# A decoder layer on one core: long GpSimd work moved to VectorE, substitution by columns, attention blocks in lockstep

## The chip, the cores and the metric

The kernel runs on one core of one Trainium2 chip. The metric is device time in microseconds (us) of one execution. A core has five engines that work from queues of their own, each strictly in its program's order: TensorE (PE, matmuls; PEld is its weight load), VectorE (DVE), ScalarE (ACT), GpSimd (POOL) and SyncE (SP, which issues all DMAs here). They wait for each other on semaphores. Matmuls write to PSUM; everything else lies in SBUF or in device memory.

## The reference

One layer on 1024 tokens of width 1024, all in float32: a half-weighted SwiGLU block, a token mixer, a second SwiGLU block, a final RMSNorm. The mixer is what matters here:

```python
qa, ka, va, qkv_b, beta_raw, decay_raw, gdn_gate, gate_a, gate_b = jnp.split(h @ w_in, offsets, axis=-1)
# branch A: 12 heads of 64, three groups: window/dilation (128,1) (512,4) (2048,16), blocks of 128 queries
s = jnp.einsum('brnqhd,brnkhd->brnhqk', qb, kw) * (Dh ** -0.5)   # masked band
p = jnp.exp(s - m); l = jnp.sum(p, axis=-1, keepdims=True)
o = jnp.einsum('brnhqk,brnkhd->brnqhd', p / l, vw); lse = m + jnp.log(l)
wts = jax.nn.softmax(jnp.stack(lses, axis=0), axis=0)            # mixes the three groups
# branch B: 8 heads of 128, causal conv of 4 taps, silu, l2norm of q and k, then in chunks:
M = jnp.where(tri_strict, jnp.einsum('bhnid,bhnjd->bhnij', kbeta, kc) * decay, 0.0)
sol = lax.linalg.triangular_solve(M + jnp.eye(C), rhs, left_side=True, lower=True, unit_diagonal=True)
v_new = u_i - w_i @ state;  o_i = q_i @ state + a_i @ v_new      # scan over the chunks
state = state * sd_i + k_i^T @ v_new
ob = rmsnorm(ob, gdn_out_norm) * jax.nn.silu(gdn_gate)
merged = sigmoid(gate_a) * (ya @ w_branch_a) + sigmoid(gate_b) * (yb @ w_branch_b); return merged @ w_out
```

## The kernel before, in words

The stages run one after the other: first feed-forward (0 to 735 us), mixer (735 to 1930), merge of the branches and w_out (1930 to 2110), second feed-forward (2110 to 2878). Long products are made from pairs of a rounded high part and a low part: a weight tile arrives by DMA in `wraw`, ScalarE casts it to `wH` (L181), and the low part `wL` = `wraw` - `wH` is made on L182. Each product of 128 output columns by 512 tokens takes 24 matmuls of 128x512 (L204, in `proj`). In the mixer `C.pool_split` sends the low parts of the DeltaNet heads and gates to GpSimd, 48 tiles; the others go to VectorE.

The mixer is one long stream of such projections, 3072 long matmuls, into which everything else is woven. `Weave` keeps a planned time: `fill` adds 0.23 for each long matmul, and as soon as 2.07 (`STRETCH`, nine of them) have passed since the last poll, `poll` runs every task whose due time is reached. A task is a generator; the number that it yields is its delay until its next step. Matmuls keep this order on PE (`keep_in_program_order`). On the other engines a list scheduler places the instructions, by bands of priority: attention first, then heads 0 to 7, and the bulk (casts and low parts) last. PE therefore has one fixed order, and if an operand is late, all of PE waits.

What is woven in:

- `attention_block`, 48 blocks (3 groups, 2 pairs of heads, 8 blocks). Step one: two score products (L772), masked row maximum on VectorE (L774), exponential on ScalarE (L779). Step two, 2.07 later: transposes (L787) and their copies. Step three, 2.07 later: product with the values (L799), copy to the tile `o`, DMA to device memory. A block's first step is due 10.0 + 3.8 b after its projections.
- `combine`, eight times: reads the three groups' outputs back, mixes them on VectorE (L830 to L845), transposes on PE (L849) 9 planned us later.
- For each head of branch B: `gdn_conv` (L899 to L902, four taps: one on ScalarE, three on VectorE), `by_token` (transposes L908, squares L918, sums L919), `gdn_decay` (the masks D, L974 to L977), `gdn_solve`, `gdn_values` and `gdn_scan` over eight chunks of 128 (L1187: product with the state, L1189: subtraction on VectorE, L1191, L1197, L1202: state update on VectorE, nine long matmuls between turnarounds), `gdn_output` (L1224 to L1229).
- `rsqrt_cols` makes an inverse square root by three Newton steps. In the mixer three callers hand it `nc.gpsimd`: norms of keys and queries and the output norm, 32 calls. On GpSimd a step is four operations (L163, L168, L169, L170), on VectorE three (L163, L165, L166).
- `gdn_solve` inverts the unit lower triangles. `gdn_inverse_blocks` stores the diagonal 32x32 blocks of N and reads them back as `M`, one block per lane in four copies that each take eight columns, so that all 32 blocks of a head are inverted at once: entry i of a column is the sum of the entries before it times `M`'s entries i, one multiply and one sum per i (L1061 and L1062 for 1 to 15 in both halves at once, L1066 and L1067 for 16 to 31). The result goes out and back by DMA and is transposed (L1077). `gdn_merge` joins the blocks (L1097 to L1121). Its first product is due 51 planned us (`INVERSE` - 5) after the key products; before it, two scalings of the keys (L1022) run on GpSimd.

```python
def poll(self):
    while self.tasks and self.tasks[0][0] < self.now + 0.05:
        task = heapq.heappop(self.tasks)[2]
        delay = next(task, None)
```

Of the kernel before, what the change touches and what calls it, by code (L numbers as in the profile page):

```python
# [16 lines left out]
P = 128  # L17
T = 1024
# [64 lines left out]
STRETCH = 2.07  # L83


class Weave:
# [3 lines left out]
    def __init__(self, tc):  # L90
        self.tc, self.now, self.tasks, self.n, self.busy, self.last = tc, 0.0, [], 0, False, 0.0

# [664 lines left out]
def attention_block(C, q, k, g, hp, V, b):  # L757
# [7 lines left out]
    with band(C, "att"):  # L765
        o = C.mx.tile([P, 132], F32, name="o", tag="o", bufs=3)
        nm = C.mx.tile([P, 2], F32, name="nm", tag="nm", bufs=3)
        S = []
        for h in range(2):
            rows = slice(h * 64, h * 64 + 64)  # L770
            ps = psum(C, "tC")
            pe(nc.tensor.matmul(ps[:, :nk], q[rows, b * P:b * P + P], k[rows, k0:k0 + nk], start=True, stop=True), nk * 0.0017)  # L772
            s = C.mx.tile([P, 256], F32, name="s", tag="sc", bufs=7)
# [7 lines left out]
    yield STRETCH  # L781
    with band(C, "att"):
        pTs = []
        for h in range(2):
# [3 lines left out]
            pT = C.mx.tile([P, 256], F32, name="pT", tag="sc", bufs=7)  # L788
# [5 lines left out]
    yield STRETCH  # L794
# [16 lines left out]
    C.blocks -= 1  # L811


def combine(C):

    nc = C.nc
    while C.blocks:
        yield 1.0
    yield 4.0
    for t in range(NT):  # L820
        while sum(not X.vals[1] for X in C.heads) > 1:
            yield 1.0
        oc = C.tp.tile([P, 792], F32, name="oc", tag="xs", bufs=2).rearrange("p (g q f) -> p g q f", g=3, q=2)
# [15 lines left out]
        y = C.mx.tile([P, 256], F32, name="cy", tag="sc", bufs=7)  # L839
# [3 lines left out]
        yv = y.rearrange("p (q f) -> p q f", q=2)  # L843
        nc.vector.tensor_tensor(out=yv, in0=oc[:, 0, :, 0:128], in1=oc[:, 1, :, 0:128], op=ALU.add)
        nc.vector.tensor_tensor(out=yv, in0=yv, in1=oc[:, 2, :, 0:128], op=ALU.add)  # L845
        yield 9.0
        ps = psum(C, "tA")
        for f in range(2):
            C.weave.pe(nc.tensor.transpose(ps[:, f * P:f * P + P], y[:, f * P:f * P + P], C.ident), 0.11)  # L849
        yT = C.mx.tile([P, 2, P], F32, name="yT", tag="sc", bufs=7)  # L850
# [31 lines left out]
def gdn_conv(C, w_in, c0, ti, X, out, then):  # L882
# [6 lines left out]
    for q in (0, 1):  # L889
# [13 lines left out]
        C.weave.add(in_band(C, X.band, then(q)), 7.0)  # L903
# [34 lines left out]
def gdn_queries(C, w_in, X):  # L938
    X.q = t4c(C, "ka")

    def then(q):
        by_token(C, X, X.q, q, 8, None)
        if q:
            rs, _ = rsqrt_cols(C, X.ssq[:, 8:16], 1.0, EPS, 8, "rg", C.nc.gpsimd, 24)
# [10 lines left out]
def gdn_decay(C, X):  # L955
# [4 lines left out]
    while X.prev and not (X.prev.vals[1] and X.prev.A):  # L960
        yield 0.6
    segs = []
# [16 lines left out]
    X.D = D  # L979
# [17 lines left out]
def gdn_solve(C, X):  # L997
# [5 lines left out]
    rs, sv = rsqrt_cols(C, X.ssq[:, 0:8], 1.0, EPS, 8, "rg", nc.gpsimd, 24)  # L1003
# [17 lines left out]
    for dst, sc in ((kg, C.eG[:, :, h]), (X.kd, ks)):  # L1021
        nc.gpsimd.tensor_tensor(out=dst, in0=X.kd, in1=sc.unsqueeze(2).to_broadcast([P, NT, P]), op=ALU.mult)  # L1022
# [13 lines left out]
def gdn_inverse_blocks(C, X):  # L1036
# [11 lines left out]
    nc.vector.memset(M[:, 0:T:33], 1.0)  # L1048
    Tb = C.mx.tile([P, 288], F32, name="fsT", tag="fsT", bufs=1)
    pr = C.mx.tile([P, 128], F32, name="fsP", tag="fsP", bufs=1)  # L1050
# [5 lines left out]
    for i in range(1, 32):  # L1056
        n = i + 1
        if i < 16:
            mv = Mh[:, :, i:i + 32 * i + 1:32].unsqueeze(2).to_broadcast([P, 2, 4, n])
            v = pr[:, :8 * n].rearrange("p (h x j) -> p h x j", h=2, x=4)  # L1060
            nc.vector.tensor_tensor(out=v, in0=Th[:, :, :, 0:n], in1=mv, op=ALU.mult)  # L1061
            nc.vector.tensor_reduce(out=Th[:, :, :, i], in_=v, axis=AX.X, op=ALU.add)  # L1062
        else:
            mv = M[:, i:i + 32 * i + 1:32].unsqueeze(1).to_broadcast([P, 4, n])
            v = pr[:, :4 * n].rearrange("p (x j) -> p x j", x=4)
            nc.vector.tensor_tensor(out=v, in0=Tx[:, 0:4, 0:n], in1=mv, op=ALU.mult)  # L1066
            nc.vector.tensor_reduce(out=Tx[:, 0:4, i], in_=v, axis=AX.X, op=ALU.add)  # L1067
# [13 lines left out]
def gdn_merge(C, X, Tm, Um):  # L1081
# [13 lines left out]
    for lo, hi in quads:  # L1095
        for c in range(NT):
            pe(nc.tensor.matmul(ps[hi, c * 32:c * 32 + 32], N[lo, c, hi], Tm[lo, c, lo], start=True, stop=True), 0.055)  # L1097
        nc.vector.tensor_copy(W[hi], ps[hi, :256].rearrange("p (c t) -> p c t", t=32))
    yield STRETCH
    ps = psum(C, "tM")  # L1100
    for lo, hi in quads:
        for c in range(NT):
            pe(nc.tensor.matmul(ps[hi, c * 32:c * 32 + 32], Um[hi, c, hi], W[hi, c, :], start=True, stop=True), 0.055)
        nc.vector.tensor_copy(Tm[hi, :, lo], ps[hi, :256].rearrange("p (c t) -> p c t", t=32))
# [21 lines left out]
INVERSE = 56.0  # L1126
# [39 lines left out]
def gdn_scan(C, X):  # L1166
# [6 lines left out]
    def sc(name):  # L1173
        return C.mx.tile([P, 256], F32, name=name, tag="sc", bufs=7)[:, :P]
# [42 lines left out]
def gdn_output(C, X, q):  # L1217
# [9 lines left out]
    ro, _ = rsqrt_cols(C, so[:, 4:8], 1.0 / P, EPS, 4, "ro", nc.gpsimd, 8)  # L1227
# [35 lines left out]
def mixer(C, tc, I):  # L1263
# [9 lines left out]
    with tc.tile_pool(name="mx", bufs=1) as C.mx:  # L1273
# [8 lines left out]
        C.blocks = 0  # L1282
        for g in range(3):
# [3 lines left out]
            for hp in range(2):  # L1287
                q, k = [rope_tile(C, w_in, c0 + g * 256 + hp * P, g) for c0 in (C_QA, C_KA)]
                for b in range(NT):
                    C.blocks += 1  # L1290
                    C.weave.add(attention_block(C, q, k, g, hp, V, b), 10.0 + 3.8 * b)
        C.heads = []
# [4 lines left out]
        C.pool_split = True  # L1297
# [225 lines left out]
```

## Time and profile before

| | us |
|---|---|
| median of 3 runs (2880.1 to 2881.13) | 2880.3 |
| profiled execution: its time | 2880.11 |
| profiled execution: span, first to last instruction | 2878.4 |
| PE busy / VectorE / ScalarE / GpSimd | 2694.7 / 1352.7 / 914.1 / 528.5 |
| mean granted clock of TensorE | 0.971 |

Busy time of PE is from the first to the last of overlapping matmuls, so an interval without waits reads 100%. The granted clock is the share of full speed that the throttle allowed; a stretch at 0.50 runs matmuls at half speed. In a group's row the part behind the bar is busy time, mean ns of one, then the engine's idle time before it and who ended it. In a list of waits "PE tM L787 <- ACT s L779: 11.6, 11, 4.1" says that PE stood before L787 until ScalarE's L779 was done, 11.6 us in all, 11 times, at most 4.1. A tile's row gives least, median and greatest duration in ns.

### The profile page before, as it was taken

How to read it: one execution, taken by the hardware profiler on the slowest of the kernel's cores; microseconds unless marked ns; L12 is line 12 of the kernel's file. 1: busy time of each engine (PE TensorE's matmuls, PEld its weight loads, DVE VectorE, ACT ScalarE, POOL GpSimd, SP SyncE). 2: the span in 40 equal slices, each digit the busy share in tenths (PEclk: the TensorE clock that was granted, in tenths of full speed). 3: DMA queues.
4: the chain of work that ended last, by engine and by line, in shares of the span. 5: the costliest groups of instructions: out<-in, count | busy, mean ns of one | idle time of the engine just before them, and what ended most of it. 6: DMA issues, size and time to landing. Idle time of an engine off the chain costs nothing. (4 is left out here: it accounts for less than half of the span.)

```text
span 2878.4 us, 34491 instructions
## 1 busy us (share of the span) xinstructions
PE 2694.7 (94%) x13223; PEld 2216.0 (77%) x13223; DVE 1352.7 (47%) x2830; ACT 914.1 (32%) x1570; POOL 528.5 (18%) x704
## 2 busy tenths in 40 slices
PE   6999999999899986889898888999999999999998
PEld 5888887887777765767777777788878888888886
DVE  6434344435344357747747546635653232332325
ACT  5333332213343355333344244234441111111112
POOL 5544441002000013223323223200110000000002
PEclk9999999999899998999999998999999999999999
DMA  5322225321322212212122112236431111111111
GB/s 151 92 88 84 74 81 186 101 97 66 107 61 74 59 47 76 69 47 62 42 57 55 50 50 54 81 109 203 143 107 45 52 52 44 52 51 45 44 59 59
DMA packets 276997, 221.20 MB, mean 77 GB/s; under 512 B 38144, under 2 KB 226784, under 8 KB 276832
## 3 DMA queue, kind: packets, MB, share of 16 engines
q1 hardware_dynamic: 276832, 219.00, 25.3%
q8 instruction: 104, 1.70, 0.3%
q14 instruction: 61, 0.50, 0.1%
HBM read 173.76 MB, written 38.90 MB: 74 GB/s over the span
## 5 line engine op out<-in xcount | busy, mean ns | idle before, releaser
L204 PE MATMUL mm<-hL,wH 128*128 128x512 f32 x1440 | 596.1, 414 | 0.0
L204 PE MATMUL mm<-hH,wH 128*128 128x512 f32 x1440 | 573.2, 398 | 0.0
L204 PE MATMUL mm<-hH,wL 128*128 128x512 f32 x1440 | 572.9, 398 | 0.0
L181 ACT CAST wH<-wraw 128x1024 fp32r<-128x1024 f32 (+1 forms) x189 | 197.4, 1047 | 767.2 <-PE mm L204 343.7
L204 PEld LDWEIGHTS mm<-hH,wH 128*128 128x128 f32 x1440 | 277.1, 192 | 61.9
L204 PEld LDWEIGHTS mm<-hL,wH 128*128 128x128 f32 x1440 | 278.8, 194 | 54.8 <-issue 1.9
L204 PEld LDWEIGHTS mm<-hH,wL 128*128 128x128 f32 x1440 | 278.6, 193 | 51.2
L182 DVE TENSOR_TENSOR wL<-wraw,wH 128x1024 fp32r<-128x1024 f32 (+1 forms) x141 | 171.9, 1223 | 161.9 <-ACT wH L181 159.0
L182 POOL TENSOR_TENSOR wL<-wraw,wH 128x1024 fp32r<-128x1024 f32 x48 | 116.4, 2425 | 473.1 <-ACT wH L181 464.3
L204 PE MATMUL tC<-hH,wL 128*128 128x512 f32 x416 | 161.8, 389 | 0.0
L204 PE MATMUL tC<-hL,wH 128*128 128x512 f32 x416 | 161.8, 389 | 0.0
L204 PE MATMUL tC<-hH,wH 128*128 128x512 f32 x416 | 161.8, 389 | 0.0
L1451 POOL TENSOR_TENSOR y<-x,gB 128x1024 f32<-128x1024 f32 x8 | 19.1, 2390 | 706.4 <-DVE x L292 706.4
L261 DVE TENSOR_TENSOR sg<-sg,tC 128x512 f32<-128x512 f32 x44 | 30.3, 688 | 248.0 <-PE tC L204 248.0
L237 POOL TENSOR_TENSOR xg<-x,gB 128x1024 f32<-128x1024 f32 x16 | 38.3, 2396 | 441.0 <-DVE x L568 231.0
L385 DVE TENSOR_TENSOR wL<-wS,wH 128x1024 fp32r<-128x1024 f32 x44 | 63.3, 1439 | 79.1 <-ACT wH L384 77.9
L901 DVE SCALAR_TENSOR_TENSOR ka<-xp,cw,ka 128x512 f32<-128x512 f32 x96 | 84.9, 887 | 25.0 <-ACT ka L899 24.0
L204 PEld LDWEIGHTS tC<-hH,wH 128*128 128x128 f32 x416 | 78.2, 188 | 16.2
L204 PEld LDWEIGHTS tC<-hL,wH 128*128 128x128 f32 x416 | 78.0, 188 | 16.2
L204 PEld LDWEIGHTS tC<-hH,wL 128*128 128x128 f32 x416 | 78.0, 187 | 16.2
L376 POOL TENSOR_TENSOR wS<-wraw 128x512 f32<-128x512 f32 x44 | 56.3, 1301 | 136.7 <-DVE wL L385 136.7
L453 POOL TENSOR_TENSOR su<-su,sg 128x512 f32<-128x512 f32 x42 | 64.4, 1552 | 86.5 <-DVE su L427 76.7
(409 smaller groups left out, 5544.8 us busy)
## 6 DMA issues: line engine op xcount, KB each, us to landing
wraw<-in_w_in_dram SPq DMA_DIRECT2D x64, 512.0 KB, 4.0
wraw<-in_ffn_w_gate_dram SPq DMA_DIRECT2D x46, 512.0 KB, 3.9
wraw<-in_ffn_w_up_dram SPq DMA_DIRECT2D x46, 512.0 KB, 4.0
wraw<-in_ffn_w_down_dram SPq DMA_DIRECT2D x44, 512.0 KB, 3.7
wraw<-hd SPq DMA_DIRECT2D x22, 512.0 KB, 4.4
hd<-su SPq DMA_DIRECT2D x42, 256.0 KB, 3.2
wraw<-in_w_branch_b_dram SPq DMA_DIRECT2D x16, 512.0 KB, 4.3
wraw<-in_w_out_dram SPq DMA_DIRECT2D x16, 512.0 KB, 4.3
```

What stands on the lines that cost most here:

```text
L181: nc.scalar.copy(H[:, :width], raw[:, :width])
L182: (nc.gpsimd if C.pool_split else nc.vector).tensor_tensor(out=L[:, :width], in0=raw[:, :width], in1=H[:, :width].bitcast(F32), op=ALU.sub ...
L204: ins = nc.tensor.matmul(ps, w[:, k, :], x[:, k, :], start=k == 0 and i == 0, stop=k == kt - 1 and i == 2)
L237: nc.gpsimd.tensor_tensor(out=xs, in0=x_t, in1=gB, op=ALU.mult)
L261: nc.vector.tensor_tensor(out=sg, in0=sg, in1=pu, op=ALU.mult)
L376: nc.gpsimd.tensor_tensor(out=out, in0=p, in1=q, op=op)
L385: eng.tensor_tensor(out=L[:, :n], in0=srcs, in1=H[:, :n].bitcast(F32), op=ALU.subtract)
L453: C.nc.gpsimd.tensor_tensor(out=out, in0=out, in1=sg, op=ALU.mult)
L901: nc.vector.scalar_tensor_tensor(o, x, w, o, op0=ALU.mult, op1=ALU.add)
L1451: nc.gpsimd.tensor_tensor(out=y, in0=x2[:, t], in1=gF, op=ALU.mult)
```

## The change

Six parts, all in the mixer.

1. The Newton chains of its 32 `rsqrt_cols` calls run on VectorE, and so do its low parts (`C.pool_split` stays false) and the two scalings of the keys, now in halves of 128x512.
2. The substitution goes by columns: entry j, once it is known, times the entries right of `M`'s diagonal in row j is added to all later entries, a multiply and an add per j, for j from 0 to 14 in both halves, then four products and reductions that carry the first 16 entries into the last 16, then j from 16 to 30: 68 operations in place of 62. `M`'s diagonal is no longer set to one.
3. `attention` steps all blocks that are under way at each poll, and starts one new block per poll; while attention lasts, the polls are 2.76 apart (`WIDE`, twelve long matmuls). A block's transposes come two polls behind its scores.
4. `combine` waits for `C.attended`, then 8 instead of 4; each of its rounds waits while a decay matrix is made (`C.segs`), which in turn waits for a round (`C.combining`), as they share a pair of buffers; its transposes follow 12 planned us later.
5. `INVERSE` is 48, a convolution's transposes are due 8 after it instead of 7.
6. In `gdn_merge` the copies come after both halves' products; `sc` has 6 buffers, `o` and `nm` have 4.

```diff
+WIDE, STRETCH = 2.76, 2.07
...
-        if self.now - self.last > STRETCH - 0.01:
+        if self.now - self.last > self.stretch - 0.01:
             self.poll()
...
-    yield STRETCH
+    yield
+    yield
     with band(C, "att"):
         pTs = []
...
+def attention(C):
+    going = []
+    while C.blocks or going or C.more:
+        going = [b for b in going if next(b, True) is None]
+        if C.blocks and C.blocks[0][0] <= C.weave.now:
+            b = C.blocks.pop(0)[1]
+            next(b)
+            going.append(b)
+        yield C.weave.stretch
+    C.attended = True
+    C.weave.stretch = STRETCH
...
 def combine(C):
-    while C.blocks:
+    while not C.attended:
         yield 1.0
-    yield 4.0
+    yield 8.0
     for t in range(NT):
-        while sum(not X.vals[1] for X in C.heads) > 1:
+        while C.segs or sum(not X.vals[1] for X in C.heads) > 1:
             yield 1.0
+        C.combining = True
...
-        yield 9.0
+        yield 12.0
...
-    rs, sv = rsqrt_cols(C, X.ssq[:, 0:8], 1.0, EPS, 8, "rg", nc.gpsimd, 24)
+    rs, sv = rsqrt_cols(C, X.ssq[:, 0:8], 1.0, EPS, 8, "rg", w=24)
...
     for dst, sc in ((kg, C.eG[:, :, h]), (X.kd, ks)):
-        nc.gpsimd.tensor_tensor(out=dst, in0=X.kd, in1=sc.unsqueeze(2).to_broadcast([P, NT, P]), op=ALU.mult)
+        for q in range(2):
+            cs = slice(q * 4, q * 4 + 4)
+            nc.vector.tensor_tensor(out=dst[:, cs], in0=X.kd[:, cs], in1=sc[:, cs].unsqueeze(2).to_broadcast([P, 4, P]), op=ALU.mult)
...
+    def step(rows, x, m, n):
+        v = pr[:, :rows.shape[1] * 4 * n].rearrange("p (h x i) -> p h x i", x=4, i=n)
+        nc.vector.tensor_tensor(out=v, in0=x, in1=m, op=ALU.mult)
+        nc.vector.tensor_tensor(out=rows, in0=rows, in1=v, op=ALU.add)
...
+    for j in range(15):
+        n = 15 - j
+        m = Mh[:, :, 33 * j + 1:33 * j + 1 + n].unsqueeze(2).to_broadcast([P, 2, 4, n])
+        step(Th[:, :, :, j + 1:16], Th[:, :, :, j:j + 1].to_broadcast([P, 2, 4, n]), m, n)
+    m = M[:, :512].rearrange("p (j i) -> p j i", i=32)[:, :, 16:]
+    for x in range(4):
+        v = pr.rearrange("p (j i) -> p j i", i=16)
+        nc.vector.tensor_tensor(out=v, in0=Tx[:, x, 0:16].unsqueeze(2).to_broadcast([P, 16, 16]), in1=m, op=ALU.mult)
+        nc.vector.tensor_reduce(out=Tx[:, x, 16:], in_=v.rearrange("p j i -> p i j"), axis=AX.X, op=ALU.add)
...
-INVERSE = 56.0
+INVERSE = 48.0
...
-                    C.weave.add(attention_block(C, q, k, g, hp, V, b), 10.0 + 3.8 * b)
+                    C.blocks.append((C.weave.now + 10.0, attention_block(C, q, k, g, hp, V, b)))
...
-        C.pool_split = True
```

What it does to the order on the engines, at three places. First PE in the attention stretch (group 0 and 1; L772 or L774 are scores, L787 or L790 transposes, L799 or L802 products with the values), before:

```order
L772 MATMUL tC<-ka 128x256 x2
L204 MATMUL mm<-hL_3503,wH 128x512
...
L799 MATMUL tA<-ka,pT 128x64 x4
L772 MATMUL tC<-ka 128x128 x2
L787 MATMUL tM<-ident,s 128x128 x4
L204 MATMUL mm<-hL_3503,wH 128x512
```

and with the change:

```order
L802 MATMUL tA<-ka,pT 128x64 x4
L790 MATMUL tM<-ident,s 128x128 x4
L774 MATMUL tC<-ka 128x128 x2
L206 MATMUL mm<-hH_4711,wL 128x512
...
L802 MATMUL tA<-ka,pT 128x64 x4
L790 MATMUL tM<-ident,s 128x128 x4
L774 MATMUL tC<-ka 128x256 x2
```

Left out are long matmuls, nine in all between two steps before, twelve now. The transposes behind the first score row are those of its own block before (nine long matmuls on) and those of an older block now; a block's own follow 24 long matmuls behind its scores.

Second VectorE where head 2's key norm is made (`rgv`, `rgy`, `rgt` are the Newton chain's tiles, `cl` the scales, `Dm` the decay matrix, `v` the scan's subtraction), before:

```order
L158 TENSOR_SCALAR rgv<-gssq 128x8
L160 TENSOR_SCALAR rgy<-rgv 128x8
L161 ISA rgy<-rgy,magic 128x16
L1189 TENSOR_TENSOR v_10152<-vb,tC 128x128
L1005 TENSOR_TENSOR cl<-rgy 128x8
```

and with the change:

```order
L163 ISA rgy<-rgy,magic 128x16
L165 TENSOR_TENSOR rgt<-rgy 128x8
L167 SCALAR_TENSOR_TENSOR rgt<-rgt,rgv 128x8
L168 SCALAR_TENSOR_TENSOR rgy<-rgt,rgy 128x8
L1220 TENSOR_TENSOR v_10150<-vb,tC 128x128
```

The nine operations between L163 and L1024 (L1005 before) now stand in VectorE's own queue, the scan's subtraction among them, where before L1005 stood at the queue's head until GpSimd had done twelve.

Third, VectorE's low part in the same place, with the change:

```order
L1028 TENSOR_TENSOR Dm<-Dm,cl 128x512 x2
L1030 TENSOR_TENSOR cl<-cl,ex 128x8
L184 TENSOR_TENSOR wL<-wraw,wH 128x1024
L919 SCALAR_TENSOR_TENSOR ka<-xp,cw,ka 128x512
L1011 SCALAR_TENSOR_TENSOR ka<-tA,Dm 128x512
```

The row L184 stood on GpSimd before; now convolution and key products queue behind it.

Counted in long matmuls of the mixer, the first transposes of `combine` stand at 943 before and 1034 now, and between a head's key products and its first merge product (L1097, now L1126) stand 207, 180, 225, 189, 216, 189, 216, 189 before and 171, 153, 189, 171, 180, 171, 180, 180 now (heads 0 to 7).

More of the change, by code (lines that the diff above doesn't have):

```diff
@@ L959, in gdn_decay @@
     h = X.h
-    while X.prev and not (X.prev.vals[1] and X.prev.A):
+    while C.combining or X.prev and not (X.prev.vals[1] and X.prev.A):
         yield 0.6
+    C.segs = True
     segs = []
@@ L1281, in mixer @@
         C.weave = Weave(tc)
-        C.blocks = 0
+        C.blocks, C.more, C.attended = [], True, False
         for g in range(3):
```

62 lines of the change are left out of this document (28 added, 34 removed).

## The prediction

> **What bounds the kernel now.** I read the page first: its header and the busy shares (PE 94%) say that TensorE is the engine to keep fed. Then the stretches: they show where it is not. Columns are the window, its length, then busy time (instructions) of PE, weight loads, VectorE, ScalarE, GpSimd, then granted clock, DMA share, GB/s.
>
> ```profile
> 802.00:1090.00 288.00, 271.82 (x1429) 212.74 (x1430) 124.71 (x384) 126.65 (x367) 21.01 (x25) 0.98 0.23 60
> 1090.00:1300.00 210.00, 165.64 (x948) 136.52 (x948) 135.59 (x375) 82.86 (x155) 52.75 (x107) 0.89 0.22 61
> 1300.00:1930.00 630.00, 569.99 (x3240) 469.47 (x3239) 371.04 (x914) 221.84 (x401) 178.46 (x371) 0.95 0.21 58
> 2300.00:2400.00 100.00, 100.00 (x443) 82.81 (x442) 31.93 (x43) 12.15 (x14) 0.00 (x0) 1.00 0.16 48
> ```
>
> The last row is the second feed-forward: 443 matmuls in 100 us, 0.226 us each, full clock. The first three are the mixer, which alone is edited. PE idles 288 - 271.8 = 16.2 us in the attention stretch, 44.4 us where attention hands over to the DeltaNet heads, 60.0 us in the heads: 121 us. On top comes the clock: (1 - 0.98) x 288 = 5.8, 0.11 x 210 = 23.1, 0.05 x 630 = 31.5 us. PE executes its program in one order and the change leaves the number of its matmuls alone, so the time can move only by these 181 us and by new waits. Third view: what PE waited for, by stretch (total, times, longest). Attention first, then hand-over, then heads:
>
> ```profile
> PE tM L787 <- ACT s L779: 11.6, 11, 4.1
> ...
> PE tA L849 <- DVE cy L845: 9.8, 2, 8.3
> PE tA L990 <- ACT sq L918: 7.0, 1, 7.0
> PE tM L1097 <- DVE Tm L1077: 6.8, 1, 6.8
> PE tC L1187 <- DVE S L1202: 4.4, 3, 2.7
> PE tA L908 <- ACT vT L902: 4.4, 1, 4.4
> PE tC L1197 <- DVE v L1189: 3.2, 2, 2.2
> PE tC L1187 <- DVE S L1200: 2.8, 1, 2.8
> ...
> PE tC L1187 <- DVE S L1202: 12.1, 11, 3.9
> PE tC L1191 <- DVE vb L1208: 8.1, 4, 3.8
> PE tM L1097 <- DVE W L1098: 4.6, 6, 2.0
> PE tA L908 <- DVE ka L992: 4.1, 1, 4.1
> PE tA L908 <- DVE fsT L1067: 4.0, 2, 2.7
> PE tA L908 <- DVE g L1236: 3.0, 1, 3.0
> PE tC L1197 <- DVE v L1189: 2.0, 4, 1.0
> ```
>
> In the heads nearly every releaser is VectorE, though its busy share there is only 371/630 = 59%. Fourth: why is an engine with spare time late? It is held up by GpSimd, in two ways: it stands in its queue until a Newton chain on GpSimd is done, and it is slowed while GpSimd works.
>
> ```profile
> DVE roy L1228 <- POOL roy L170: 43.5, 16, 3.4
> DVE cl L946 <- POOL rgy L170: 21.6, 8, 5.1
> DVE cl L1005 <- POOL rgy L170: 14.2, 5, 3.5
> ...
> 1118.04 2.40 POOL L182 TENSOR_TENSOR wL<-wraw,wH 128x1024 fp32r<-128x1024 f32 x1 [10.03 <-ACT wH L181]
> 1118.24 2.42 DVE L1066 TENSOR_TENSOR fsP<-fsT,Tm 128x104 f32<-128x104 f32 x1
> ...
> L901 DVE SCALAR_TENSOR_TENSOR ka<-xp,cw,ka 128x512 f32<-128x512 f32 x96 | 84.9, 887 | 25.0 <-ACT ka L899 24.0
> L901 DVE SCALAR_TENSOR_TENSOR vT<-xp,cw,vT 128x512 f32<-128x512 f32 x48 | 35.8, 745 | 4.6 <-ACT vT L899 4.5
> L1228 DVE TENSOR_TENSOR roy<-roy,cl 128x4 f32<-128x4 f32 x16 | 15.4, 963 | 43.5 <-POOL roy L170 43.5
> L1066 DVE TENSOR_TENSOR fsP<-fsT,Tm x128: 273/337/2473, 1110.5 to 1840.6; 128x68 f32<-128x68 f32 x8, 128x72 f32<-128x72 f32 x8, 128x76 f32<-128x76 f32 x8, 128x80 f32<-128x80 f32 x8
> L1061 DVE TENSOR_TENSOR fsP<-fsT,Tm x120: 166/302/2490, 1092.6 to 1817.6; 128x16 f32<-128x16 f32 x8, 128x24 f32<-128x24 f32 x8, 128x32 f32<-128x32 f32 x8, 128x40 f32<-128x40 f32 x8
> L1066 DVE TENSOR_TENSOR fsP<-fsT,Tm 128x68 f32<-128x68 f32 (+15 forms) x128 | 53.7, 420 | 3.1
> L1061 DVE TENSOR_TENSOR fsP<-fsT,Tm 128x16 f32<-128x16 f32 (+14 forms) x120 | 50.2, 418 | 3.1
> ```
>
> Queue waits: 43.5 + 21.6 + 14.2 = 79.3 us. The pair of timeline rows is one hit: a multiply with median 0.337 us lasted 2.42 us, until the low part on GpSimd ended. Mean against undisturbed duration gives the sum of hits: L901 (887 - 745) x 96 = 13.6, L1061 (418 - 302) x 120 = 13.9, L1066 (420 - 337) x 128 = 10.6, L1228, against some 165 ns for so small an operation, 12.8; together 51 us in four groups.
>
> **The change, part by part.**
>
> *VectorE's own ledger.* It takes over 48 low parts, 32 Newton chains of nine small operations (8 heads x keys, queries and two output halves) and 32 scalings of 128x512. Nearest rows:
>
> ```profile
> L182 DVE TENSOR_TENSOR wL<-wraw,wH 128x1024 fp32r<-128x1024 f32 (+1 forms) x20 | 23.9, 1198 | 21.5 <-ACT wH L181 19.5 <-PE mm L204 2.0
> L158 DVE TENSOR_SCALAR rgv<-gssq 128x8 f32<-128x8 f32 x16 | 2.6, 165 | 0.2
> L1229 DVE TENSOR_TENSOR vb<-vb,roy 128x512 f32<-128x512 f32 x16 | 11.0, 686 | 0.3
> L1067 DVE TENSOR_REDUCE fsT<-fsP 128x4 f32<-128x68 f32 (+15 forms) x128 | 32.6, 254 | 3.0
> L1062 DVE TENSOR_REDUCE fsT<-fsP 128x8 f32<-128x16 f32 (+14 forms) x120 | 27.4, 228 | 3.0
> L844 DVE TENSOR_TENSOR cy<-oc 128x256 f32<-128x256 f32 x8 | 3.3, 419 | 0.1
> ```
>
> 48 x 1.20 = 57.5, 288 x 0.165 = 47.5, 32 x 0.686 = 22: +127 us. Away go 51 us of hits and 79.3 us of queue waits: about -3. But a low part on VectorE waits at the head of its queue for ScalarE's cast: 21.5/20 = 1.07 us each so far, up to 51 us for 48. So VectorE is held between 3 us less and 48 us more than now; what improves is the grain: 1.2 us pieces instead of 2.4 us hits and 2.7 us waits (43.5/16).
>
> *Substitution.* Before, undisturbed: 15 x (0.302 + 0.228) + 16 x (0.337 + 0.254) = 17.4 us per head. Now 30 operations of 8 to 120 elements (L1061's median as upper bound: 9.1), four products and four reductions of 256 (L844: 8 x 0.42 = 3.4), 30 of 4 to 60 elements (between L1061's least and its median, I take 0.22: 6.6): at most 19.1. Columns are worth nothing by themselves, 0 to +2 us per head; no term.
>
> *A, attention.* Scores and transposes of a block stand nine or so matmuls apart today, 24 tomorrow (one empty step): 15 x 0.226 = 3.4 us more room against a longest wait of 4.1, so nearly all of the 11.6 us goes: -11, and in proportion 11/16.2 of the 5.8 us of clock: -4. Copies to PV get 12 instead of 9. Bounds: -22 (all) to +3 (a score step late for its o tile). **-15.**
>
> *B, hand-over.* The combination's transposes move behind 12 us of planned work instead of 9 and its start from matmul 943 to 1034, out of head 0's substitution: of 9.8 us -8. The norm wait on L918 (a ScalarE step behind convolution work on VectorE): -5 of 7.0. Scan waits (4.4 + 3.2 + 2.8 = 10.4), half: -5. Others -2. -20 idle; of the clock 20/44.4 x 23.1 = -10. Bounds 0 to -52 (VectorE's 27 us in these rows and the norm wait in full, 34, with clock 18). **-30.**
>
> *C, heads.* The scan's waits 12.1 + 8.1 + 2.0 come at turnarounds with nine matmuls (2.03 us) of room, which one hit of 2.4 us alone exceeds: two thirds, -15; of the other VectorE waits (4.6 + 4.1 + 4.0 + 3.0 = 15.7) under half, -7. Clock 22/60 x 31.5 = -11. Bounds 0 to -64 (42 us of VectorE waits, with clock 22). **-33.**
>
> *D, what VectorE's new work costs PE.* In 840 us of heads, 48 x 1.2 us meet 7% of 112 scan turnarounds, 8 x 0.6 us = 5; eight bursts of four scalings, 4 x 0.686 = 2.7 us before the merge, 1 us each: 8; their clock 5. Bounds 0 to +51 (all cast waits reach PE). **+18.**
>
> *E, the shorter inverse.* By the order, the first merge product comes on average 27 matmuls sooner after the head's key products, 6.1 us. The inverse gets shorter by its share of hits (24.5/8 = 3.1 us) and of queue waits (a third of 79.3/8: 3.3), longer by two low parts (2.4) and a third of four chains (1.9): 2.1 us net. So 4 us of reserve go per head; today one head in eight waits (the 6.8 us row). Bounds -7 to +32 (4 us for each); I take half of the heads late by 1.5 us, with clock **+8.**
>
> Sum: -15 - 30 - 33 + 18 + 8 = **-52 us** against the profiled execution's 2880.1 us (span 2878.4, median 2880.3): **2828 us.**
>
> The clock terms rest on one observation, here in the attention stretch: after a wait of 2.31 us the next 3.4 us run at half clock.
>
> ```profile
> 1013.14 0.86 PE L787 MATMUL tM<-ident,s 128*128 128x128 f32 x2 [2.31 <-ACT s L779]
> 1012.90:1016.30 3.40, 3.15 (x8) 2.44 (x9) 0.94 (x2) 0.84 (x5) 0.00 (x0) 0.50 0.68 186
> ```
>
> The Trainium skill, page "TensorE: Matmul & The Clock Gate", section "What's actually happening", has the slow state begin after an idle window of about 3.4 us; this trace disagrees, 2.3 us were enough. By the page only the long waits would buy clock back and C's clock part would be about half, an estimate of 2833 us.
>
> **The rivals.** *More goes (R3):* every wait that names VectorE falls, in the hand-over 9.8 + 6.8 + 4.4 + 3.2 + 2.8 = 27, in the heads some 42, with clock 27/44.4 x 23.1 + 42/60 x 31.5 = 36; with A -15 and E +8: 2768. For it: VectorE is undisturbed for the first time. Against: it carries 127 us more. *Handed on (R2):* the hits go, but the next late engine is ScalarE, which itself queues casts, squares and exponentials; only A and the combination (8, clock 4) remain: 2853. For it: L918 and L902 already appear among the releasers. *Slower (R1):* the low part at the head of VectorE's queue. While it waits for the cast (1.07 us) and runs (1.20), the scan's subtraction and state update stand behind it, 2.27 us against 2.03 us of room. If half of the 51 us reaches PE and B and C bring nothing, 2880 - 15 + 26 = 2891; with A and the combination against E (-15 - 8 + 8) it decides from 15 us, 0.3 us per low part. Against: low parts stand right where the cast is due, with ready work ahead. The Trainium skill, "Perfetto Trace Analysis", section "Optimizing Scalar/DVE Operations", advises to take work off a saturated VectorE, even onto GpSimd; this change goes the other way, and 59% busy is not saturated. *It doesn't do what it says:* waits for GpSimd stay (masks of the decay matrix), 2878; the order shows the chains on VectorE, so little.
>
> **How the numbers follow.** Forecast (2800 to 2853) 50%, R3 15%, R2 17%, R1 13%, no effect 5%. The range leaves a little of R3 and most of R1 out: 2768 to 2880. A measurement here tells 0.2%, 6 us, from nothing. Faster: 50 + 15 + 15 = 80%; same: 5 + 2 = 7%; slower 13%.
>
> **What would show it.** A: the wait of the block's transposes (now L790) on L781 under 2 us in total. B: the combination's transposes (L866) no longer wait; clock above 0.92 in the hand-over. C: no VectorE operation of 2.4 us, no wait on GpSimd's chains; waits of L1218 and L1222 under 10 us together. D: low parts (L184) idle about 1 us each before them. E: L1126 waits for L1106 at up to half of the heads, under 3 us each. Wrong if PE's waits only change their releaser from VectorE to ScalarE at the same sum, or if L184's waits head the list of VectorE's idle time and the scan's waits grow.

## The result, and the profile after it

The changed kernel takes 2792.6 us, the kernel before 2880.2 us in the same comparison: a ratio of 0.9695 with a 95% interval of 0.9678 to 0.9712, or 88 us less. The profiled execution is 2792.5 us long, its span 2790.6 us. The prediction said 2828 us. The direction is right and the time lies inside the range of 2768 to 2880 us, but 7 us below the forecast's own 2800 to 2853, towards the rival R3. The 35 us between 2828 and the measured time are not noise: as the experiments show, the gains were a little over twice as large as predicted, and one cost was more than five times as large.

For the comparison by stages the windows are cut where PE executes the same long matmul of the mixer in both kernels (numbers 0, 864, 1349, 2700 and 3060): attention, hand-over, heads, last head. Columns: window, its length, busy time (instructions) of PE, weight loads, VectorE, ScalarE, GpSimd, then granted clock, DMA share, GB/s. The kernel before:

```profile
768.80:1081.90 313.10, 296.92 (x1539) 233.20 (x1538) 138.96 (x417) 135.21 (x386) 18.50 (x23) 0.98 0.25 65
1081.90:1302.80 220.90, 176.12 (x1007) 145.48 (x1006) 140.23 (x383) 90.24 (x169) 57.81 (x113) 0.90 0.22 62
1302.80:1813.00 510.20, 458.22 (x2611) 377.50 (x2609) 319.88 (x777) 192.84 (x350) 156.38 (x315) 0.95 0.20 53
1813.00:1929.40 116.40, 108.80 (x610) 89.31 (x608) 49.30 (x137) 27.90 (x48) 19.53 (x52) 0.99 0.26 82
```

The kernel after:

```profile
771.40:1049.00 277.60, 277.40 (x1483) 223.05 (x1482) 138.80 (x400) 126.75 (x362) 2.53 (x6) 1.00 0.27 72
1049.00:1256.30 207.30, 176.10 (x1068) 147.61 (x1067) 152.07 (x517) 100.34 (x195) 7.43 (x14) 0.92 0.26 69
1256.30:1735.90 479.60, 445.68 (x2657) 376.24 (x2656) 347.05 (x1130) 202.55 (x363) 13.97 (x34) 0.95 0.21 56
1735.90:1844.60 108.70, 101.17 (x559) 84.42 (x558) 34.71 (x82) 30.34 (x48) 0.00 (x0) 0.95 0.35 112
```

The four stretches are 35.5, 13.6, 30.6 and 7.7 us shorter; a part of the first difference is work that moved, as 56 of its matmuls (x1539 to x1483) now run in the later stretches. In the first, PE's idle time is gone (277.60 - 277.40 = 0.2 us against 16.2) and its clock is full. In the other three it still idles 31, 34 and 7.5 us, 73 us of the 104 before, and the clock in the heads is 0.95 as before: most of the idle time there is still lost. The second view says to whom. It is what PE waited for in the mixer after the change (total, times, longest); the chain from the diagonal blocks to L1106, the transposition that ends the inverse, has become nearly the only cause:

```profile
PE tM L1126 <- DVE Tm L1106: 53.5, 7, 18.5
PE mm L663 <- ACT wH L183: 6.1, 1, 6.1
PE tA L866 <- DVE ka L1011: 4.8, 1, 4.8
PE tA L926 <- ACT ka L920: 4.1, 2, 2.3
```

No wait of a block's transposes (L790) and none of the scan (L1218, L1222, L1228) is left among them. The third view, VectorE's groups of the substitution and of the low parts, says why. Durations are minimum/median/maximum in ns, then first and last start; the last row has busy time, mean, and the idle time ahead with its cause:

```profile
L1077 DVE TENSOR_TENSOR fsP<-fsT,Tm x240: 157/200/283, 1071.1 to 1734.7; 128x56 f32<-128x56 f32 x16, 128x40 f32<-128x40 f32 x16, 128x24 f32<-128x24 f32 x16, 128x8 f32<-128x8 f32 x16
L1091 DVE TENSOR_REDUCE fsT<-fsP x32: 568/595/624, 1084.3 to 1724.8; 128x16 f32<-128x256 f32 x32
...
L184 DVE TENSOR_TENSOR wL<-wraw,wH 128x1024 fp32r<-128x1024 f32 (+2 forms) x81 | 97.9, 1211 | 78.4 <-ACT wH L183 70.2 <-PE mm L206 5.6 <-PE tA L926 2.4
```

The longest multiply of the columns is now 0.283 us, where a hit before made one of the rows last 2.4 us; no operation of VectorE in the mixer lasts over 1.25 us. VectorE stands 70 us ahead of low parts waiting for ScalarE's casts, and of PE's waits in these 1195 us a low part is named for 0.2 us in all.

Theory 1, formed from this: the undisturbed VectorE was worth more than the prediction gave it, and the shorter inverse (`INVERSE` 56 to 48) cost far more than its +8. Its rivals: the head chain would be the bound whatever the due time; or the gain lies in attention, the columns or the small edits.

### The profile page after: what moved, and what is told of

Its sections match the earlier page's. It is cut to its first block, busy times and chain, and to the rows that moved or that the text cites. A ratio compares the mean times of both kernels' runs of the same rounds, so it can differ in the third digit from the quotient of the medians.

```text
span 2790.6 us, 34448 instructions
## 1 busy us (share of the span) xinstructions
PE 2652.4 (95%) x13223; PEld 2199.6 (79%) x13223; DVE 1371.2 (49%) x3238; ACT 920.3 (33%) x1574; POOL 300.1 (11%) x256
## 5 line engine op out<-in xcount | busy, mean ns | idle before, releaser
L206 PE MATMUL mm<-hH,wL 128*128 128x512 f32 x1440 | 589.9, 410 | 0.0
L206 PE MATMUL mm<-hL,wH 128*128 128x512 f32 x1440 | 567.5, 394 | 0.0
L206 PE MATMUL mm<-hH,wH 128*128 128x512 f32 x1440 | 567.4, 394 | 0.0
L184 DVE TENSOR_TENSOR wL<-wraw,wH 128x1024 fp32r<-128x1024 f32 (+1 forms) x189 | 230.5, 1222 | 213.9 <-ACT wH L183 204.8
L206 PEld LDWEIGHTS mm<-hL,wH 128*128 128x128 f32 x1440 | 273.9, 190 | 60.7
L206 PEld LDWEIGHTS mm<-hH,wH 128*128 128x128 f32 x1440 | 274.8, 191 | 50.4
L206 PEld LDWEIGHTS tC<-hH,wL 128*128 128x128 f32 x416 | 78.2, 188 | 16.2
L919 DVE SCALAR_TENSOR_TENSOR ka<-xp,cw,ka 128x512 f32<-128x512 f32 x96 | 72.5, 755 | 13.1 <-ACT ka L917 11.9
L386 ACT CAST wH<-wS 128x1024 fp32r<-128x1024 f32 x44 | 46.3, 1052 | 78.1 <-PE tC L397 37.5
L568 PE MATMUL mm<-wH,hidH 128*128 128x512 f32 x176 | 69.3, 394 | 2.6 <-DVE x L570 1.8
```

The lines of the kernel that those rows point to most:

```text
L184: (nc.gpsimd if C.pool_split else nc.vector).tensor_tensor(out=L[:, :width], in0=raw[:, :width], in1=H[:, :width].bitcast(F32), op=ALU.sub ...
L206: ins = nc.tensor.matmul(ps, w[:, k, :], x[:, k, :], start=k == 0 and i == 0, stop=k == kt - 1 and i == 2)
L386: nc.scalar.copy(H[:, :n], srcs)
L568: nc.tensor.matmul(ps, h[:, m], w, start=i == 0, stop=i == len(seq) - 1)
L919: nc.vector.scalar_tensor_tensor(o, x, w, o, op0=ALU.mult, op1=ALU.add)
```

## The experiments

Each was measured beside the kernel before; ratios are to that kernel, with 95% intervals. 1% is 28.8 us. Lines have other numbers where a kernel's text is longer or shorter.

### The due time of the inverse

The change with the old due time:

```
-INVERSE = 48.0
+INVERSE = 56.0
```

> The change with INVERSE back at 56: the merge is due 8 planned us later, all else as changed. Theory 1 (the substitution's latency is the one wait left on TensorE, 53.5 us at L1126, because the due time was cut by more than the chain got shorter): the seven waits of 18.5, 1.5, 9.7, 2.5, 9.3, 4.8 and 7.2 us lose up to 8 us each, about 40 us in all, and half-clock time with them; 2735 to 2755 us, L1126 under 16 us. Rival (the chain of a head, inverse, merge, scan, next head, is the bound, so a later merge only moves the wait behind it): 2785 to 2800 us, with the wait at the scan or at the next head's values.

Measured: 2748.3 us, ratio 0.9541 (0.9523 to 0.9558). This beats both kernels. Its windows from the hand-over on, cut at the same matmuls, and its waits of PE:

```profile
1049.60:1247.80 198.20, 172.46 (x1063) 144.42 (x1061) 151.25 (x512) 97.57 (x193) 6.87 (x14) 0.95 0.26 71
1247.80:1693.80 446.00, 432.26 (x2613) 363.69 (x2612) 331.97 (x1026) 192.41 (x350) 13.92 (x34) 0.98 0.23 61
1693.80:1800.20 106.40, 104.73 (x610) 88.14 (x609) 55.19 (x185) 27.83 (x48) 0.00 (x0) 1.00 0.28 87
```

```profile
PE tM L1126 <- DVE Tm L1106: 10.6, 1, 10.6
PE tA L926 <- ACT ka L920: 8.7, 4, 3.7
PE mm L663 <- ACT wH L183: 6.6, 1, 6.6
```

One edited number takes 43 us of waits for the inverse away (53.5 to 10.6) and the time falls by 44. So the shorter due time costs 1.54% inside the change. Is that a cost of its own? The kernel before with the new due time:

```
-INVERSE = 56.0
+INVERSE = 48.0
```

> The kernel before with INVERSE 48 in place of 56, nothing else. Theory 1 (the shorter inverse is a cost of its own, 44 us inside the change, because the head's chain from gates to inverse is then the last to end): slower than before, 2895 to 2930 us, waits of the first merge product on VectorE's T (L1097 on L1077) of 40 us or more against 12.4 us. Rival (it costs only because the change's heads are packed more tightly; before, VectorE's hits set the end and the due time matters little): 2875 to 2890 us.

Measured: 2889.0 us, ratio 1.0045 (1.0028 to 1.0062). Theory 1 as written falls, and the rival's range (2875 to 2890 us) holds: the same edit costs 13 us there, under a third. The waits of the merge product on the inverse grew only from 6.8 to 14.1 us in this view of the mixer:

```profile
PE tC L1187 <- DVE S L1202: 17.0, 8, 5.3
PE tM L1097 <- DVE Tm L1077: 14.1, 5, 5.4
```

So the price depends on what stands around it. Two more due times, 52 and 60, in the change:

> The change with INVERSE 52. From the run with 56, the time that each head's T lay ready before its first merge product was 14.7, 0, 6.5, 1.3, 5.4, 2.3, 4.0, 2.6 us, and head 1 waited 10.6. Theory 1 (each head loses the 4 us one for one): L1126 waits 18 to 22 us in total over heads 1, 3, 5 and 7, time 2755 to 2768 us. Rival (the loss grows only at 48, because something else ends the chain below 52): L1126 within 3 us of 10.6, 2743 to 2752 us.

Measured: 2772.7 us, ratio 0.9632 (0.9616 to 0.9649), with

```profile
PE tM L1126 <- DVE Tm L1106: 32.9, 5, 12.7
```

The rival falls; theory 1 has the direction, but the wait is 33 us and not 18 to 22, and the time lies above its 2755 to 2768. Taking 4 us from each head's reserve is not enough: the chain itself got longer (below); why it did was not taken apart.

> The change with INVERSE 60. Theory 1 (at 56 only head 1's first merge product is late, by 10.6 us): waits of L1126 under 4 us and 2735 to 2748 us. Rival (a longer inverse only pushes each head's end later, so that the scan of the last heads runs with less work beside it): 2750 to 2765 us with the waits on ScalarE and GpSimd grown at the program's later heads.

Measured: 2760.7 us, ratio 0.9590 (0.9576 to 0.9605), 12 us above the run with 56 (14 by the ratios). Theory 1 falls. The rival's time holds, and its waits in part (ScalarE and VectorE, not GpSimd). The wait of head 1's first merge product stays at 11.0 us, so a later due time does not remove it (its cause stays open), and behind the last head PE now waits for the finished head and its projection, with nothing left to fill in. PE's waits from 1796 us on:

```profile
PE tA L926 <- DVE vb L1260: 6.1, 1, 6.1
PE mm L206 <- ACT mH L213: 4.1, 1, 4.1
```

In the run with 56 the first of these is missing and the second is 0.4 us.

**Where the head's time goes.** Head 3 in the three kernels: the stores of its diagonal blocks (SyncE's queue, four of them), the transposition that ends the inverse, the first merge product, each with first and last start behind the durations. Before:

```profile
L1044 SPq DMA_DIRECT2D nbd<-ka x4: 328/442/449, 1388.2 to 1389.6; - x4
L1077 DVE STREAM_TRANSPOSE Tm<-U x1: 1245/1245/1245, 1446.0 to 1446.0; 128x1024 f32<-128x1024 f32 x1
L1097 PE MATMUL tM<-Tm,ka x32: 191/191/212, 1453.5 to 1455.2; 32*32 32x32 f32 x32
```

After:

```profile
L1065 SPq DMA_DIRECT2D nbd<-ka x4: 303/450/1601, 1333.7 to 1336.2; - x4
L1106 DVE STREAM_TRANSPOSE Tm<-U x1: 1245/1245/1245, 1390.7 to 1390.7; 128x1024 f32<-128x1024 f32 x1
L1126 PE MATMUL tM<-Tm,ka x32: 236/236/258, 1392.0 to 1393.5; 32*32 32x32 f32 x32
```

The change with 56:

```profile
L1065 SPq DMA_DIRECT2D nbd<-ka x4: 327/450/1742, 1321.2 to 1322.6; - x4
L1106 DVE STREAM_TRANSPOSE Tm<-U x1: 1245/1245/1245, 1374.0 to 1374.0; 128x1024 f32<-128x1024 f32 x1
L1126 PE MATMUL tM<-Tm,ka x32: 191/191/212, 1376.6 to 1377.5; 32*32 32x32 f32 x32
```

From the last store to the end of the transposition is the chain: 57.6, 55.8 and 52.7 us. From the last store to the first product is the cover that PE's other work gives it: 63.9 us before, 54.0 with 56; after the change PE came 9.6 us early, at 46.2, and waited. The same reading over heads 2 to 7, means in us (long matmuls counted between last store and product):

| kernel | chain | first product at | of it waiting | long matmuls between |
|---|---|---|---|---|
| before | 58.1 | 63.4 | 0 | 192 |
| before, with 48 | 57.8 | 58.1 | 1.4 | 167 |
| small edits and attention, 56 (below) | 57.9 | 60.7 | 0 | 192 |
| change, with 56 | 50.4 | 54.0 | 0 | 192 |
| change, with 52 | 53.2 | 55.1 | 3.4 | 183 |
| change (48) | 52.6 | 52.7 | 5.8 | 169 |

The rows with 192 long matmuls hold the answer. The number between the two points is the same before and in the change with 56, and yet the cover fell by 9.4 us: in these windows PE idled 5.9 us and spent 6.0 us at half clock before (3.0 us lost), 0.4 and 0 us in the change with 56. PE's other waits had been part of the inverse's cover. The third row, a run told below that leaves the GpSimd part and the substitution as they were, shows that the small edits and attention take only 2.7 us of the 9.4; the other 6.7 us, and the shorter chain, come with the GpSimd part (with rows in place of columns the change with 56 has 50.9 and 53.8 us). The due time is counted in planned work, and once PE does that work without stalls, the same due time is 9 us shorter.

### GpSimd's work, put back in pieces

Low parts of the heads and gates back on GpSimd, all else as changed:

```
         heads, C.heads = C.heads, []
+        C.pool_split = True
```

> The change with the 48 low parts back on GpSimd, TensorE's order unchanged. Theory 1 (GpSimd's long operations hold VectorE up): single VectorE operations of 2.4 us come back, some 50 us of them in sum, the waits at the scan (L1218, L1222, L1228) come back with 15 to 25 us, L1126 grows; 2815 to 2830 us. Rival (the low parts were harmless there, and on VectorE they cost 48 x 1.2 us): 2770 to 2795 us.

Measured: 2823.3 us, ratio 0.9802 (0.9785 to 0.9818), 31 us above the change, as theory 1 had it. Its waits hold only in part: L1218 and L1228 come back with 5.2 us and not 15 to 25, and L1126 does not grow (51.0 us); PE's idle time in the heads rises from 33.9 to 52.8 us over many small waits. The hits are back, in the substitution's two-input multiplies and sums; the reduction, with one input, is spared (compare L1091 after the change, above), though 6 of its 32 executions overlap a low part on GpSimd:

```profile
L1077 DVE TENSOR_TENSOR fsP<-fsT,Tm x240: 156/203/2397, 1067.5 to 1763.2; 128x56 f32<-128x56 f32 x16, 128x40 f32<-128x40 f32 x16, 128x24 f32<-128x24 f32 x16, 128x8 f32<-128x8 f32 x16
L1078 DVE TENSOR_TENSOR fsT<-fsT,fsP x240: 156/202/2457, 1067.8 to 1763.4; 128x56 f32<-128x56 f32 x16, 128x40 f32<-128x40 f32 x16, 128x24 f32<-128x24 f32 x16, 128x8 f32<-128x8 f32 x16
L1091 DVE TENSOR_REDUCE fsT<-fsP x32: 569/594/620, 1081.0 to 1752.8; 128x16 f32<-128x256 f32 x32
```

The Trainium skill, page "SBUF — State Buffer", section "Who interferes with whom", says that a VectorE instruction with two SBUF inputs contends with a GpSimd instruction that reads SBUF, and that a reduction does not on trn2. These rows agree: 2.397 and 2.457 us against 0.620 us as the longest.

The Newton chains back on GpSimd (the third caller, the queries' norm, likewise):

```
...
-    rs, sv = rsqrt_cols(C, X.ssq[:, 0:8], 1.0, EPS, 8, "rg", w=24)
+    rs, sv = rsqrt_cols(C, X.ssq[:, 0:8], 1.0, EPS, 8, "rg", C.nc.gpsimd, 24)
...
-    ro, _ = rsqrt_cols(C, so[:, 4:8], 1.0 / P, EPS, 4, "ro", w=8)
+    ro, _ = rsqrt_cols(C, so[:, 4:8], 1.0 / P, EPS, 4, "ro", C.nc.gpsimd, 8)
```

> The change with the 32 Newton chains back on GpSimd, low parts and scaling on VectorE. Theory 1: VectorE stands about 2.7 us at the head of its queue for each chain, 80 us in sum, but without low parts on GpSimd no longer behind a 2.4 us operation; TensorE loses 10 to 20 us, 2803 to 2813 us. Rival (the queue waits fall into VectorE's spare time): within 5 us of 2793.

Measured: 2831.9 us, ratio 0.9834 (0.9813 to 0.9855): 39 us above the change, twice what theory 1 gave. VectorE's waits, in its own list:

```profile
DVE roy L1259 <- POOL roy L172: 40.6, 16, 3.4
...
DVE cl L1024 <- POOL rgy L172: 24.9, 8, 3.4
```

Two rows alone are 65 us at the head of VectorE's queue, for 24 chains. In the change, nine operations of some 0.17 us each on VectorE, 1.5 us, stand in place of a wait of 2.7 us on average. PE sees it at the scan, where the change has no wait, and at the inverse:

```profile
PE tM L1126 <- DVE Tm L1106: 60.4, 7, 19.0
PE tC L1218 <- DVE S L1233: 11.5, 7, 3.3
```

Both of these runs, low parts and Newton chains, have the due time of 48, at which PE waits for the inverse in seven of the eight heads; there a longer chain of a head counts at once (its mean over heads 2 to 7 is 55.1 us with the low parts back, 57.5 us with the Newton chains back, 52.6 us in the change). So 31 and 39 us are prices beside that due time; with 56 the two were not tried one by one.

All of it back (low parts, chains and the scalings of the keys), with `INVERSE` 56 so that the inverse does not cover the difference:

> The change without its GpSimd part: low parts, Newton chains and the scaling are back on GpSimd, INVERSE is 56 as before; columns, attention and the combine stay as changed. Theory 1 (the freed VectorE carries the gain; the low parts alone cost 31 us and the Newton chains 39 us when put back, attention 4): 2845 to 2870 us, within some 35 us of the kernel before, with VectorE's 2.4-us operations and its waits on GpSimd's chains back and waits of the scan on VectorE of over 10 us. Rival (the other parts, columns and stepping together, carry much of it, and the two single runs overlap): 2800 to 2825 us.

Measured: 2816.4 us, ratio 0.9788 (0.9773 to 0.9802), 68 us above the change with 56 (71 by the ratios). Here theory 1's number fails and the rival's holds: the change keeps 61 us without its GpSimd part. The next runs look for them.

### Attention, columns and the small edits

The change's attention undone (own due times, steps 2.07 planned us apart), `INVERSE` 48:

```
-        self.stretch = WIDE
+        self.stretch = STRETCH
...
+                    C.weave.add(attention_block(C, q, k, g, hp, V, b), 10.0 + 3.8 * b)
```

> The change with attention as before: each block its own task, steps 2.07 apart, polls every nine matmuls; all else as changed. Theory 1 (attention is worth the prediction's term, some 15 us, and what the first stretch gained beyond it comes from VectorE): 2805 to 2815 us, with 10 to 15 us of waits of the transposes for the exponential. Rival (the lockstep carries the gain): 2830 us or more.

Measured: 2796.8 us, ratio 0.9713 (0.9693 to 0.9733): 4 us, inside the uncertainty. Both expectations fail. Taken alone this run says that attention is worth almost nothing. It is a run in which heads wait 49 us for the inverse, though, as they do in the change: the first stretch, with 59 more matmuls in it, is 22 us longer than in the change, the hand-over and the heads together 20 us shorter (299.8, 194.6 and 472.2 us against 277.6, 207.3 and 479.6). Its waits:

```profile
PE tM L1112 <- DVE Tm L1092: 49.2, 8, 12.4
...
PE tM L789 <- ACT s L781: 2.6, 7, 1.1
```

So attention was tried again with `INVERSE` 56. Substitution by rows first, to see what columns bring (`INVERSE` 56 too):

```
+    for i in range(1, 32):
+        n = i + 1
...
+            nc.vector.tensor_tensor(out=v, in0=Tx[:, 0:4, 0:n], in1=mv, op=ALU.mult)
+            nc.vector.tensor_reduce(out=Tx[:, 0:4, i], in_=v, axis=AX.X, op=ALU.add)
```

> The change with INVERSE 56 and the substitution by rows, as before, in place of columns. Theory 1 (columns shorten a head's substitution by about 1.3 us of 17.4 and this only shows where the first merge product waits, 10.6 us at one head): within 0 to 15 us of the change with INVERSE 56, 2745 to 2763 us, waits of L1126's successor on VectorE's T of 10 to 25 us. Rival (columns carry gain through fewer long operations on VectorE): 2770 us or more.

Measured: 2745.5 us, ratio 0.9542 (0.9528 to 0.9556), against 0.9541 by columns: no difference that can be measured. The rest is settled by four runs with rows and `INVERSE` 56, which hold the small edits and, of attention and the GpSimd part, neither, one, the other, or both (the run by rows just told). The small edits:

```
-    yield 4.0
+    yield 8.0
...
-        yield 9.0
+        yield 12.0
...
-    while X.prev and not (X.prev.vals[1] and X.prev.A):
+    while C.combining or X.prev and not (X.prev.vals[1] and X.prev.A):
```

> The kernel before with only the small edits: combination without its own tile and 12 us later, a head's keys and decay stage held until the combination's transposes are through, the keys' start at 8.0, copies of the two quads split, inverse still 56; attention, rows, and all work on GpSimd as before. Theory 1 (these edits are worth the combination's wait of 9.8 us and its clock): 2862 to 2876 us. Rival (they carry a large part of the 61 us by which the change without its GpSimd part beats the kernel before): 2850 us or less, with the hand-over stretch at least 15 us shorter.

Measured: 2865.5 us, ratio 0.9954 (0.9939 to 0.9969). Theory 1's number holds, but not its reason. The hand-over stretch is as long as before; the attention stretch is 8 us shorter, with 4.8 us of waits of the transposes against 11.6, and the heads and the last head together are 7 us shorter (619.9 against 626.6 us):

```profile
768.90:1073.90 305.00, 293.24 (x1539) 231.50 (x1538) 140.19 (x417) 134.96 (x386) 18.48 (x23) 0.99 0.25 66
1073.90:1294.70 220.80, 176.54 (x1003) 143.79 (x1002) 143.14 (x393) 89.83 (x169) 60.26 (x114) 0.90 0.24 65
1294.70:1813.00 518.30, 459.56 (x2658) 378.71 (x2657) 329.66 (x828) 202.69 (x364) 158.01 (x325) 0.95 0.19 52
1813.00:1914.60 101.60, 100.22 (x565) 82.90 (x564) 35.68 (x82) 28.08 (x47) 16.67 (x40) 1.00 0.33 108
```

Which of these edits does it (a fourth `o` tile is among them) was not taken apart. Attention's blocks stepping together on top of that (the function `attention` of the change's diff):

> The run of the small edits plus attention's blocks that step together; rows, inverse 56 and all work on GpSimd as before. Theory 1 (with the inverse at 56 the 16.2 us of waits and half of 13.7 us at half clock in the attention stretch stay won): 15 to 30 us below the run of the small edits alone, no wait of the transposes. Rival (attention's gain is given back in the heads, as when only 4 us were lost by undoing it with inverse 48): within 8 us of that run. Columns, by the difference to the change without its GpSimd part (2816): 2811 to 2831 if they are worth 0 to 2 us per head either way.

Measured: 2821.2 us, ratio 0.9799 (0.9784 to 0.9814), 1.55% or 45 us below the small edits alone, more than both theories. Columns again show nothing: the run of all work on GpSimd, which differs from this one by columns alone, stands at 0.9788, 3 us below, within the intervals. The same windows:

```profile
771.80:1049.40 277.60, 277.40 (x1482) 223.07 (x1481) 134.49 (x383) 126.84 (x362) 18.23 (x21) 1.00 0.27 72
1049.40:1263.60 214.20, 176.15 (x1063) 145.09 (x1062) 145.21 (x416) 99.65 (x195) 58.81 (x114) 0.94 0.24 66
1263.60:1759.20 495.60, 450.78 (x2612) 374.86 (x2611) 313.99 (x771) 189.85 (x348) 157.38 (x317) 0.95 0.20 55
```

The attention stretch is 27 us shorter and without idle time, though 57 of its instructions have moved to later stretches. The heads gain too (idle 58.7 to 44.8 us), where no attention runs any more. The steps also shift what stands beside the scans there; why that helps was not taken apart. Last, the GpSimd part without stepping blocks:

> The run of the small edits plus the GpSimd part (low parts, Newton chains, scaling on VectorE); attention as before, rows, inverse 56. Theory 1 (parts add up: the GpSimd part is worth the 68 us that it is worth beside the stepping blocks): 60 to 76 us below the run of the small edits alone. Rival (the parts need each other: with attention's blocks at odd times VectorE cannot use its freedom): 20 to 50 us below it, with waits of the transposes and of the scan on VectorE left.

Measured: 2767.5 us, ratio 0.9617 (0.9602 to 0.9631), 3.37% or 97 us below the small edits alone. The rival falls, and so does theory 1's number. With the run of both, the square is:

| ratio to before | blocks at own times | blocks step together |
|---|---|---|
| work on GpSimd | 0.9954 | 0.9799 |
| work on VectorE | 0.9617 | 0.9542 |

Either part brings more without the other: attention 45 us or 22, the GpSimd part 97 us or 74. Some 23 us can be had by either; that these are the same waits was not shown.

## Why the prediction came out as it did

The ledger in the prediction's own terms, against what the runs give when the parts are added in this order (in us: a difference of ratios times 2880):

| term of the prediction | predicted | measured | from |
|---|---|---|---|
| small edits (combination, of B: -8 and 4 of clock) | -12 | -13 | 1 to 0.9954 |
| A, attention | -15 | -45 (-22 beside the GpSimd part) | 0.9954 to 0.9799 |
| rest of B, C and D, the GpSimd part | -18 - 33 + 18 = -33 | -74 (-97 alone) | 0.9799 to 0.9542 |
| columns | 0 | 0 | 0.9542 to 0.9541 |
| E, the shorter inverse | +8 | +44 | 0.9541 to 0.9695 |
| sum | -52 | -88 | |

**E failed**, and most plainly. Its step was "4 us of reserve go per head", from 6.1 us less cover by the order and a chain 2.1 us shorter. The count of matmuls was near (27 fewer predicted over all heads; 192 to 169 in the table, for heads 2 to 7), and the chain gained more than I gave it (58.1 to 52.6 us). What the ledger lacked is that the change's own gains, C's above all, shorten the cover: 9.4 us of it per head had for the most part been PE's idle time and slow clock. Cover fell from 63.4 to 46.9 us (52.7 less the 5.8 of waiting), 16.5 us, the chain by 5.5; the reserve was 5.3 us, so the heads come 5.7 us late, and 5.8 is what they wait. Seven heads wait, for 1.5 to 18.5 us, where E had up to half of them, under 3 us each. Head 1, with the 18.5, is outside this account: it waits 6.8 us before and 10.6 us in the change with 56, and why stays open. The kernel before shows the other half: there, the same edit cost 13 us. The ledger priced each stall by itself and never asked what all of them together had been covering.

**C and the rest of B were too small.** I took two thirds of the scan's waits and under half of the others. After the change no scan wait is left, as R3 had said, and with `INVERSE` 56 PE's idle time in the heads falls from 510.2 - 458.2 = 52.0 us at a clock of 0.95 to 446.0 - 432.3 = 13.7 us at 0.98. R3's own parts without E come to 2760 us; the change with 56 takes 2748. So R3 had the gains nearly right, and missed the time through E. The halving had no row behind it: the trace of before showed VectorE 59% busy, and nothing in it that would keep VectorE late once both causes were gone.

**D does not appear.** VectorE idles 0.97 us before each low part (78.4 / 81), 0.87 us of it for the cast, near the 1.07 of the prediction; yet PE waits for one for 0.2 us in all, the scan, where D put a part of its cost, does not wait at all, and no wait of PE names the scalings (L1043): nothing of the +18 is seen. R1 falls with it. That the head of the queue is held where VectorE has time would fit this; it was not shown.

**A was right in place, wrong in size.** The transposes' wait is gone altogether and the attention stretch runs at full clock, 16 us of idle time less where the term had 11. Beside the freed VectorE it is worth 22 us, at its lower bound; more alone, in stretches that I had not counted; and 4 us where the heads wait for the inverse anyway.

**B** is right in sum for the combination and not in mechanism: L866 still waits 4.8 us (9.8 before), and the small edits gain in attention and from the heads on instead. The clock of the hand-over is 0.92, at the mark and not above it, and 0.95 with 56.

**R2**, the waits handed on to ScalarE, falls: with 56 the waits of L926 and L663 on ScalarE, 8.7 and 6.6 us, head what is left beside head 1, but all waits of PE in the mixer that name ScalarE add up to 28 us, against 48 before.

So that the time fell into the range is in part luck, by errors of opposite sign: some 72 us too little gain, 36 us too little cost.

## What to carry to other kernels

A due time that is counted in work shrinks in microseconds when the work beside it stops stalling, here by 9 us of 63; when stalls are removed, re-time it, and do not shorten it unmeasured in the same edit. Price parts in each other's presence: the same undone part cost 4, 22 or 45 us, depending on which wait stood behind it. If an engine is late although it has time, count the instructions that wait at the head of its queue and those that last as long as a neighbour's, and ask what would keep it late once both causes are gone: here all of the scan's waits went, not two thirds.

## What was not expected of the hardware

A wait of 1.54 us was followed by half clock. PE's timeline after the change, and the windows behind it:

```profile
1306.09 1.09 PE L1126 MATMUL tM<-Tm,ka 32*32 32x32 f32 x32 [1.54 <-DVE Tm L1106]
```

```profile
1304.00:1307.40 3.40, 1.86 (x36) 1.40 (x35) 1.42 (x2) 3.36 (x5) 0.64 (x1) 1.00 0.06 10
1307.40:1310.80 3.40, 3.40 (x9) 2.58 (x9) 1.90 (x3) 1.19 (x2) 0.00 (x0) 0.50 0.05 10
1310.80:1314.20 3.40, 3.40 (x45) 2.82 (x44) 1.58 (x4) 1.07 (x2) 0.00 (x0) 0.99 0.52 149
```

So a wait need not reach the 2.31 us of the prediction's observation; the 32 small products behind this wait may count as little work, which was not tried. Nor is every wait of this size followed by half clock: behind waits of 1.75 us (at 1255.7 us, after the change) and of 2.33 us (at 1228.4 us, in the change with 56) the next 3.4 us ran at 1.00. What decides it is open. In a long wait, on the other hand, most of the slow time costs nothing, since it lies within the wait itself: in the 18.5 us of head 1 the clock is at half for 14.5 us without work and for 6.0 us of work after it.

```profile
1166.90:1170.90 4.00, 0.05 (x1) 0.00 (x0) 4.00 (x27) 0.00 (x0) 0.00 (x0) 1.00 0.48 131
1170.90:1185.40 14.50, 0.00 (x0) 0.00 (x0) 5.95 (x25) 0.00 (x0) 0.40 (x1) 0.50 0.12 19
1185.40:1191.40 6.00, 5.98 (x44) 5.24 (x45) 1.13 (x3) 0.40 (x2) 0.00 (x0) 0.50 0.00 0
```

So the short wait cost more clock per microsecond of waiting than the long one, 3.4 us at half clock behind 1.54 us against 6.0 us behind 18.5; the prediction's clock terms, in proportion to idle time, leave that out.
